# Attention scores on one core: output tiles of one head by four rows in place of two heads by eight

## The chip, the core and the metric

The kernel runs on one core of a Trainium2 chip. The core has a matrix engine (PE, TensorE), a vector engine (DVE, VectorE), a scalar engine (ACT, ScalarE), GpSimd (POOL), a queue engine that issues DMAs (SP, SyncE), and 16 DMA engines that move data between its on-chip memory and the chip's main memory. The metric is the device time of one execution in microseconds, lower is better. Before the change it is 205.95 us, the median of 3 runs (205.71 to 206.01).

## What is computed

For 8 batches and 8 heads, with 512 rows of 64 numbers each in q and k, all in float32, the kernel computes the scaled products of every row of q with every row of k:

```python
batch, heads, seq, dim = 8, 8, 512, 64
scale = 1.0 / np.sqrt(q.shape[-1])
return (np.einsum('bhqd,bhkd->bhqk', q, k) * scale).astype(np.float32)
```

The inputs are 16.8 MB together, the output is 67.1 MB.

## The kernel before

The work goes batch by batch. `load` (lines 53 to 58) brings k and q of one batch into two tiles of 1 MB: partition (g m) holds 16 consecutive rows (R = 16) of head g, and the same rows of head g + 4 (the index x is 0 or 1 for the two halves of the heads), so each partition receives two runs of 4 KB. Four batches (AHEAD = 4) are loaded ahead; the load of batch b + 4 is issued after the first pair of stores of batch b (line 131).

Then the data is cast to bf16 (line 87), on VectorE and ScalarE for the first batch and on GpSimd for all others. The cast puts the two heads of a pair side by side, so that one 128x128 transpose on PE (lines 95 and 103) turns both at once: afterwards partitions 0 to 63 hold the 64 numbers of head g and partitions 64 to 127 those of head g + 4. Eight transposes fill one PSUM tile, which VectorE copies into kT (line 97) and ScalarE into qT (line 105).

RO is the number of consecutive output rows that one partition of an output tile holds. All of these follow from it: HP = RO * 128 / 512, the number of heads that share the 128 partitions of an output tile; U = 128 / HP, the partitions per head; JJ = 16 / RO, how a query row is numbered inside qT; and IW = 8 / JJ, the rows i of qT that one copy fills. With RO = 8 they are HP = 2, U = 64, JJ = 2, IW = 4.

The matmuls (line 119) take a 64-row, U-column block of qT as weights and stream the 512 columns of kT. `tile_position` says which part of the 128x128 array is used: x chooses the upper or the lower 64 rows, h the columns. With U = 64 four matmuls cover the four quarters of the array. Two PSUM tiles of 128 x 2 x 512 are filled per step, one for each x; ScalarE evacuates and scales the first (line 71), VectorE the second (line 73). There are three such PSUM buffers, and two for the transposes.

Each pass over g0 (two heads for each x) fills two output tiles of 2 MB, one for each x, and then issues two stores (line 128) on SP's queue. There are six output buffers. A framework places the waits and orders the instructions of each engine from the data that they read and write; all DMAs stand on the one queue of SP in the order of the program.

Of the kernel before, what the change touches and what calls it, by code (L numbers as in the profile page):

```python
# [1 line left out]

# [5 lines left out]


@with_exitstack  # L10
def kernel(
    ctx: ExitStack,
    tc: tile.TileContext,
    q: bass.AP,
    k: bass.AP,
    out: bass.AP,
):

    nc = tc.nc
    B, H, S, D = q.shape
    scale = 1.0 / (D ** 0.5)
    P = 128
    G = H // 2
    M = P // G
    R = S // M
    RO = 8  # L30
    HP = RO * P // S
    U = P // HP
    JJ = R // RO

    f32 = mybir.dt.float32
    bf16 = mybir.dt.bfloat16

    q_r = q.rearrange("b (x g) (m j) d -> b (g m) x (j d)", x=2, j=R)
    k_r = k.rearrange("b (x g) (m j) d -> b (g m) x (j d)", x=2, j=R)
    out_r = out.rearrange("b (x n h) (u i) k -> b x n (h u) i k", x=2, h=HP, i=RO)  # L40

    consts = ctx.enter_context(tc.tile_pool(name="consts", bufs=1))
    raw_pool = ctx.enter_context(tc.tile_pool(name="raw", bufs=4))
    bf_pool = ctx.enter_context(tc.tile_pool(name="bf", bufs=2))
    t_pool = ctx.enter_context(tc.tile_pool(name="t", bufs=2))
    out_pool = ctx.enter_context(tc.tile_pool(name="out", bufs=6))
    tpsum_pool = ctx.enter_context(tc.tile_pool(name="tpsum", bufs=2, space=bass.MemoryType.PSUM))
    psum_pool = ctx.enter_context(tc.tile_pool(name="psum", bufs=3, space=bass.MemoryType.PSUM))

    AHEAD = 4  # L50
    raws = {}

    def load(b):
        kf = raw_pool.tile([P, 2, R * D], f32, name="kf")
        qf = raw_pool.tile([P, 2, R * D], f32, name="qf")
        nc.sync.dma_start(out=kf, in_=k_r[b])  # L56
        nc.sync.dma_start(out=qf, in_=q_r[b])
        raws[b] = (qf, kf)

    load(0)  # L60
    identity = consts.tile([P, P], dtype=bf16)
    make_identity(nc, identity)
    for b in range(1, AHEAD):
        load(b)

    n_evac = 0

    def evacuate(dst, src):
        nonlocal n_evac
        if n_evac % 2 == 0:  # L70
            nc.scalar.mul(out=dst, in_=src, mul=scale)  # L71
        else:
            nc.vector.tensor_scalar(out=dst, in0=src, scalar1=scale, scalar2=None,  # L73
                                    op0=mybir.AluOpType.mult)
        n_evac += 1

    for b in range(B):
        qf, kf = raws.pop(b)
        kb = bf_pool.tile([P, R, 2, D], bf16, name="kb")
        qb = bf_pool.tile([P, R, 2, D], bf16, name="qb")  # L80
        for slab, dst in ((kf, kb), (qf, qb)):
            for x in range(2):
                if b > 0:
                    copy = nc.gpsimd.tensor_copy
                else:
                    copy = (nc.vector.tensor_copy, nc.scalar.copy)[x]
                copy(out=dst[:, :, x, :], in_=slab[:, x].rearrange("p (j d) -> p j d", j=R))  # L87


        kT = t_pool.tile([P, P, R], bf16, name="kT")  # L90
        qT = t_pool.tile([P, RO, P, JJ], bf16, name="qT")
        for j0 in range(0, R, 8):
            tp = tpsum_pool.tile([P, 8, P], bf16, name="tp")
            for j in range(8):
                nc.tensor.transpose(out=tp[:, j, :], identity=identity,  # L95
                                    in_=kb[:, j0 + j].rearrange("p x d -> p (x d)"))
            nc.vector.tensor_copy(out=kT[:, :, j0:j0 + 8], in_=tp.rearrange("d j p -> d p j"))  # L97
        IW = 8 // JJ
        for i0 in range(0, RO, IW):
            tp = tpsum_pool.tile([P, IW, JJ, P], bf16, name="tp")  # L100
            for i in range(IW):
                for jj in range(JJ):
                    nc.tensor.transpose(out=tp[:, i, jj, :], identity=identity,  # L103
                                        in_=qb[:, RO * jj + i0 + i].rearrange("p x d -> p (x d)"))
            nc.scalar.copy(out=qT[:, i0:i0 + IW], in_=tp.rearrange("d i jj p -> d i p jj"))  # L105

        kTh = kT.rearrange("d (g m) j -> d g (m j)", g=G)
        qTh = qT.rearrange("d i (g m) jj -> d i g (m jj)", g=G)
        for g0 in range(0, G, 2):
            os = [out_pool.tile([P, 2 // HP, RO, S], f32, name="o") for _ in range(2)]  # L110
            for n in range(2 // HP):
                for i in range(0, RO, 2):
                    pss = [psum_pool.tile([P, 2, S], f32, name="ps") for _ in range(2)]
                    for w in range(2):
                        for h in range(HP):
                            g = g0 + n * HP + h
                            for x in range(2):
                                rows = slice(x * D, (x + 1) * D)
                                nc.tensor.matmul(out=pss[x][h * U:(h + 1) * U, w, :],  # L119
                                                 lhsT=qTh[rows, i + w, g, :],  # L120
                                                 rhs=kTh[rows, g, :],
                                                 start=True, stop=True,
                                                 tile_position=(x * D, h * U))
                    for x in range(2):
                        evacuate(os[x][:, n, i:i + 2, :], pss[x])
            for x in range(2):
                n0 = g0 // HP
                nc.sync.dma_start(  # L128
                    out=out_r[b, x, n0:n0 + 2 // HP].rearrange("n p i k -> p n (i k)"),
                    in_=os[x].rearrange("p n i k -> p n (i k)"))  # L130
            if g0 == 0 and b + AHEAD < B:
                load(b + AHEAD)


# [1 line left out]
_INS = ['q', 'k']  # L136
_OUTS = [((8, 8, 512, 512), 'float32')]


# [23 lines left out]
```

## Time and profile before

| what | value |
|---|---|
| median of 3 runs | 205.95 us |
| the profiled execution's own time | 205.95 us |
| its span | 204.0 us |
| instructions | 1911 |
| PE / VectorE / ScalarE / GpSimd busy | 63% / 46% / 41% / 14% of the span |
| DMA queue of SP | 8960 packets, 83.89 MB, 97.6% of 16 engines' span |
| a store of 2 MB, issue to landing | 24.8 us (32 of them) |
| a load of 1 MB, issue to landing | 17.2 us for k, 19.6 us for q (8 each) |

The page is taken from one execution. Its slices divide the span into 40 equal parts; a digit is the busy share in tenths. A group of instructions reads "line engine operation, out<-in, shapes, count | busy us, mean ns of one | idle time before them <- what ended it". A line of waits reads "engine, tile, line <- what it waited for: us in total, times, longest". The rows of a stretch give its start and end, its length, the busy us of PE, PE's weight loads, VectorE, ScalarE and GpSimd with their number of instructions, the granted clock of PE as a share of full speed, the mean busy share of the 16 DMA engines, and the rate at which they moved data. Busy shares are averages over stages; what a stage is worth is read from the wait that ends last in it.

### The profile page before, as it was taken

To read this page: it belongs to the slowest core of one execution; us is meant where nothing else is said; L and a number is where in the kernel's file an instruction comes from. 1 tells how busy PE (TensorE), PEld (TensorE's weight loads), DVE (VectorE), ACT (ScalarE), POOL (GpSimd) and SP (SyncE) were. 2 spreads that over 40 slices of the span, in tenths; PEclk is the share of its full clock that TensorE was granted. 3 is DMA by queue.
4 is the path that set the end of the run, shared out by engine and by line. 5 is a ranking of instruction groups with operands and counts; after the bars stand their busy time and mean duration, and the time that the engine had idled before them with its cause. 6 is when DMAs were issued, how large, how long until landed. Compare 5 with 4: busy or idle time off the path is not lost.

```text
span 204.0 us, 1911 instructions
## 1 busy us (share of the span) xinstructions
PE 128.7 (63%) x768; PEld 44.1 (22%) x768; DVE 94.4 (46%) x82; ACT 82.8 (41%) x83; POOL 29.0 (14%) x34
## 2 busy tenths in 40 slices
PE   0398877774969559696586955959787777600000
PEld 0353433260103411033110431103211111000000
DVE  0459895912639035490536705367628081800000
ACT  2477888263522625227252452527552525200000
POOL 1077530520006100070001600000000000000000
PEclk9999999666555855558555575555555555555555
DMA  5999999999999999999999999999999999999991
GB/s 204 419 409 411 439 427 404 441 434 424 437 400 432 440 421 419 434 429 427 440 407 414 438 427 437 427 421 437 424 430 437 426 434 424 430 437 427 434 408 61
DMA packets 8969, 84.01 MB, mean 412 GB/s; under 512 B 768, under 2 KB 768, under 8 KB 4864
## 3 DMA queue, kind: packets, MB, share of 16 engines
q1 hardware_dynamic: 8960, 83.89, 97.6%
q8 instruction: 6, 0.10, 0.2%
q14 instruction: 3, 0.02, 0.0%
HBM read 16.78 MB, written 67.11 MB: 411 GB/s over the span
## 4 chain that ended last, share of the span: by engine, by line
DMA 61%; DVE 14%; PE 6%; ACT 6%; issue 1%; SPq 0%; DVEq 0%
DMA out_dram<-o 57%; DVE o L73 11%; PE ps L119 4%; ACT o L71 4%; DMA qf<-in_q_dram 3%; DVE kT L97 3%; ACT qT L105 1%; PE tp L103 1%; PE tp L95 0%; DVE qb L87 0%; SPq L56 0%; SPq L128 0%; DVEq L73 0%
## 5 line engine op out<-in xcount | busy, mean ns | idle before, releaser
L119 PE MATMUL ps<-kT,qT 64*64 64x512 bf16 x512 | 103.1, 556 | 38.6 <-ACT o L71 24.9
L73 DVE TENSOR_SCALAR o<-ps 128x1024 f32<-128x1024 f32 x64 | 75.2, 1219 | 76.7 <-DMA out_dram<-o 56.8
L71 ACT ACTIVATE o<-ps 128x1024 f32<-128x1024 f32 x64 | 64.5, 1025 | 77.1 <-PE ps L119 65.7
L119 PEld LDWEIGHTS <-qT 64*64 64x64 bf16 x512 | 22.4, 124 | 111.5 <-issue 108.6
L87 POOL CAST kb<-kf 128x1024 bf16<-128x1024 f32 x14 | 14.2, 1040 | 80.9 <-DMA kf<-in_k_dram 80.3
L105 ACT COPY qT<-tp 128x1024 bf16<-128x1024 bf16 x16 | 16.1, 1015 | 12.6 <-PE tp L103 12.4
L97 DVE COPY kT<-tp 128x1024 bf16<-128x1024 bf16 x16 | 18.9, 1215 | 0.0
L95 PE MATMUL tp<-identity,kb 128*128 128x128 bf16 x128 | 12.4, 257 | 8.0 <-ACT kb L87 6.9
L103 PE MATMUL tp<-identity,qb 128*128 128x128 bf16 x128 | 14.9, 284 | 2.2 <-DVE kT L97 1.4
L87 POOL CAST qb<-qf 128x1024 bf16<-128x1024 f32 x14 | 14.2, 1040 | 6.4 <-DMA qf<-in_q_dram 6.4
L103 PEld LDWEIGHTS <-qb 128*128 128x128 bf16 x128 | 11.7, 130 | 9.6 <-issue 8.6
L95 PEld LDWEIGHTS <-kb 128*128 128x128 bf16 x128 | 10.4, 118 | 11.4 <-ACT kb L87 6.9
L87 DVE CAST kb<-kf 128x1024 bf16<-128x1024 f32 x1 | 0.7, 694 | 5.8 <-DMA kf<-in_k_dram 5.8
L87 ACT CAST kb<-kf 128x1024 bf16<-128x1024 f32 x1 | 1.0, 1044 | 3.8 <-DMA kf<-in_k_dram 3.8
L87 ACT CAST qb<-qf 128x1024 bf16<-128x1024 f32 x1 | 1.0, 1044 | 1.5 <-DMA qf<-in_q_dram 1.5
L87 ACT ACT_TABLE_LOAD x1 | 1.3, 1283 | 0.7 <-PEq L147 0.7
L87 DVE CAST qb<-qf 128x1024 bf16<-128x1024 f32 x1 | 0.7, 695 | 1.9 <-DMA qf<-in_q_dram 1.9
masks.py:199 POOL TENSOR_SCALAR_AFFINE_SELECT identity<-identity 128x128 bf16<-128x128 bf16 x1 | 0.3, 292 | 0.1
masks.py:197 POOL MEMSET identity<- 128x128 bf16 x1 | 0.2, 204 | 0.3 <-POOLq L147 0.3
L147 POOL MEMSET const-float32-0.0<- 128x1 f32 x1 | 0.1, 98 | 0.2 <-issue 0.2
L147 POOL MEMSET const-bfloat16-1.0<- 128x1 bf16 x1 | 0.1, 101 | 0.0
L147 POOL MEMSET const-uint8-127<- 128x1 uint8 x1 | 0.1, 101 | 0.0
(1 smaller groups left out, 0.1 us busy)
## 6 DMA issues: line engine op xcount, KB each, us to landing
out_dram<-o SPq DMA_DIRECT2D x32, 2048.0 KB, 24.8
kf<-in_k_dram SPq DMA_DIRECT2D x8, 1024.0 KB, 17.2
qf<-in_q_dram SPq DMA_DIRECT2D x8, 1024.0 KB, 19.6
```

The costliest lines, as they stand in the source:

```text
L71: nc.scalar.mul(out=dst, in_=src, mul=scale)
L73: nc.vector.tensor_scalar(out=dst, in0=src, scalar1=scale, scalar2=None, op0=mybir.AluOpType.mult)
L87: copy(out=dst[:, :, x, :], in_=slab[:, x].rearrange("p (j d) -> p j d", j=R))
L95: nc.tensor.transpose(out=tp[:, j, :], identity=identity, in_=kb[:, j0 + j].rearrange("p x d -> p (x d)"))
L97: nc.vector.tensor_copy(out=kT[:, :, j0:j0 + 8], in_=tp.rearrange("d j p -> d p j"))
L103: nc.tensor.transpose(out=tp[:, i, jj, :], identity=identity, in_=qb[:, RO * jj + i0 + i].rearrange("p x d -> p (x d)"))
L105: nc.scalar.copy(out=qT[:, i0:i0 + IW], in_=tp.rearrange("d i jj p -> d i p jj"))
L119: nc.tensor.matmul(out=pss[x][h * U:(h + 1) * U, w, :], lhsT=qTh[rows, i + w, g, :], rhs=kTh[rows, g, :], start=True, stop=True, tile_posi ...
L147: nc = _bacc.Bacc("TRN2", target_bir_lowering=False, num_devices=1)
```

## The change

One constant is changed:

```diff
-    RO = 8
+    RO = 4
```

All else follows from it. HP becomes 1, U 128, JJ 4 and IW 2. An output tile is 128 x 2 x 4 x 512 in place of 128 x 1 x 8 x 512: the same 2 MB, but the two heads of a pass stand one behind the other in each partition, four rows (8 KB) of each, where before each half of the partitions held eight rows (16 KB) of one head. A store therefore writes 256 runs of 8 KB in place of 128 runs of 16 KB. The loop over n now runs twice and the loop over i over 0 and 2 in place of 0, 2, 4 and 6, so the number of steps (four in a pass) and of evacuations stays. The weights of a matmul are 64 rows by 128 columns in place of 64 by 64, so a step has four matmuls in place of eight, each on one half of the array. In qT the index jj has 4 values in place of 2, and one copy fills 2 values of i in place of 4; the number and size of the copies stay.

## The prediction

> **What bounds the kernel now.** I read the page's 40 slices first, then the DMA packets and queue, then the chain, and last the waits, to see who is early and who is late.
>
> ```profile
> DMA  5999999999999999999999999999999999999991
> GB/s 204 419 409 411 439 427 404 441 434 424 437 400 432 440 421 419 434 429 427 440 407 414 438 427 437 427 421 437 424 430 437 426 434 424 430 437 427 434 408 61
> DMA packets 8969, 84.01 MB, mean 412 GB/s; under 512 B 768, under 2 KB 768, under 8 KB 4864
> q1 hardware_dynamic: 8960, 83.89, 97.6%
> ```
>
> The DMA row is full from the second slice to the last but one: the 16 DMA engines are never out of work. The queue's 8960 packets take 97.6% of 16 engines' span. They divide into 768 tiny ones (16 completion marks for each of 48 transfers), 4096 under 8 KB (the loads: 16 x 128 partitions x 2 runs of 4 KB) and the rest, 4096 store runs of 16 KB.
>
> ```profile
> DMA out_dram<-o 57%; DVE o L73 11%; PE ps L119 4%; ACT o L71 4%; DMA qf<-in_q_dram 3%; DVE kT L97 3%; ACT qT L105 1%; PE tp L103 1%; PE tp L95 0%; DVE qb L87 0%; SPq L56 0%; SPq L128 0%; DVEq L73 0%
> L119 PE MATMUL ps<-kT,qT 64*64 64x512 bf16 x512 | 103.1, 556 | 38.6 <-ACT o L71 24.9
> L73 DVE TENSOR_SCALAR o<-ps 128x1024 f32<-128x1024 f32 x64 | 75.2, 1219 | 76.7 <-DMA out_dram<-o 56.8
> POOL kb L87 <- DMA kf<-in_k_dram: 80.3, 6, 20.0
> DVE o L73 <- DMA out_dram<-o: 56.8, 11, 8.7
> ```
>
> The chain (first line) is mostly stores, and the waits (last two) say the same from the other side: VectorE stands 56.8 us because the output buffers are still being stored, and GpSimd 80.3 us because loads queue behind stores. The 14% of evacuation in the chain is no compute bound: it is the refill after a buffer comes free, with other stores still in flight above it. So what counts is how long the 16 engines need for their packets, and the moments at the two ends when they have none. The third view is the busy time in chosen stretches:
>
> ```profile
> core 0: us, PE busy (x) PEld busy (x) DVE busy (x) ACT busy (x) POOL busy (x), PEclk, DMA share, GB/s
> 4.00:22.00 18.00, 12.62 (x128) 7.68 (x128) 12.14 (x12) 11.23 (x12) 8.80 (x9) 1.00 1.03 413
> 120.00:190.00 70.00, 42.97 (x196) 9.85 (x195) 30.53 (x26) 25.67 (x26) 0.00 (x0) 0.52 1.01 430
> 197.00:200.00 3.00, 0.00 (x0) 0.00 (x0) 0.00 (x0) 0.00 (x0) 0.00 (x0) 0.50 0.66 284
> 200.00:204.00 4.00, 0.00 (x0) 0.00 (x0) 0.00 (x0) 0.00 (x0) 0.00 (x0) 0.50 0.10 41
> ```
>
> The first stretch holds loads alone (4 KB packets), the second stores alone (16 KB). Both are gapless (a share over 1 is packets that overlap a little), yet 413 GB/s against 430: **the size of a packet has a price here.** The last two rows show that the engines don't end together: from 197 us the share falls, and some engines go on for 4 us more. By the landings of the last store the 16 engines finish 4.4 us apart, and the latest one sets the end.
>
> **The change, part by part.**
>
> *Store runs.* With RO = 4 a partition of an output tile holds two runs of 4 rows (8 KB), one for each of two heads, in place of one run of 16 KB. Still 32 stores of 2 MB, but 8192 packets for 4096. Per engine: 256 packets of 16 KB become 512 of 8 KB, 256 more. What does one more packet cost? In the trace's packet records the median 16 KB store takes 611 ns and the median 4 KB load 159 ns. If a packet is a fixed part a plus bytes at one rate, 4 x 159 - 611 = 25 = 3a, so a = 8.3 ns and 8 KB take (611 + 8.3) / 2 = 310 ns. The rates agree: 4096 x 16 / 413 = 158.7 and 16384 x 16 / 430 = 609.6 give a = 8.4. There is a third witness: of the eight 8 KB packets in the trace (instruction fetches, another queue) the shortest take 309 ns. So 256 x 8.3 ns = **+2.1 us**. No cover hides it, because the DMA engines are what everything waits for. Bounds, as no row shows an 8 KB store: below, the fixed part may belong to loads only, 0 us. Above, the means (163.9 and 612.9 ns) give a = (4 x 163.9 - 612.9) / 3 = 14.2 ns, +3.6 us; the far end is the median of the eight fetches, 352 ns: 256 x (2 x 352 - 611) = +24 us, but those ran between others' packets. I take 2.1, as two rates and the 309 ns agree on it.
>
> [...]
>
> *Latest engine.* One engine's store packets take some 15 ns more than 611 while the compute engines run, about 3.3 us by the end, and instruction fetches delay single engines by 0.3 to 1 us each; thus the 4.4 us. The matmul line falls from 512 matmuls and 512 weight loads to 256 of each, so the program from 1911 to about 1400 instructions. If what slows that engine goes with the instruction count, it loses 27% of 3.3 = 0.9 us; but the next latest engine ends only 0.8 us sooner, so the gain ends there unless it loses a fetch too. Bounds 0 and -1.2; I take **-0.3**, nearer to nothing, as no row shows what slows it.
>
> *Matmuls.* Per pair of evacuations 8 matmuls on quarters of the array become 4 on halves. Before, four start within 10 ns of each other, and the next four 427 ns later at the low clock. Eight take 0.63 us in one place and 1.08 in another:
>
> ```profile
> 17.18 0.63 PE L119 MATMUL ps<-kT,qT 64*64 64x512 bf16 x8 [0.37 <-ACT o L71]
> 18.89 0.84 SPq L128 DMA_DIRECT2D out_dram<-o  x2
> 145.62 1.08 PE ps L119 x8
> ```
>
> Two halves side by side stream as many columns, so the same 1.1 us. No row shows halves. Bound above: nothing overlaps, 4 x 0.43 + 4 x 0.13 of weight load + 0.2 = 2.4 us. A batch is 8 such groups and 32 transposes (16 take 2.10 us in the timeline): 8 x 2.4 + 4.2 = 23.4 us. Its DMA takes 8.39 MB at 430 and 2.10 MB at 413 GB/s: 19.5 + 5.1 = 24.6 us. Even so it is hidden in steady state. At the start, the first two stores are issued at 18.89 us, while 8.39 MB of loads at 413 GB/s last from 2.3 to 22.6: 3.7 us of cover, against 4 x (2.4 - 1.1) = 5.2 in that worst case, so at most 1.5 us lost. By likely overlap: 0. The other way, a faster start gains nothing: the engines are still loading.
>
> *Copies and evacuations.* qT is written in groups of 4 rather than 2, kT as before; 64 + 64 evacuations of 128x1024 stay. ACT's 1.015 us copy may move by some tenths; 16 of them lie in 77 us of idle ScalarE. The built order puts the second batch's first kT and qT copies behind the first four evacuations, which brings the first store forward by about one 1.2 us copy; the loads in flight cover that. Cost 0.
>
> *SyncE.* A store carries 256 runs, as a load does (median issue 0.49 us for a store's 0.34): 32 x 0.15 us on a queue that mostly waits. Issue blocks sooner if the queue counts packets, but then work is queued by definition. Cost 0.
>
> Sum, against the profiled execution's own 205.95 us (span 204.0, which is also the median of the three runs): 205.95 + 2.1 - 0.3 = **207.8 us**.
>
> **Rivals.**
>
> *The halves cost nothing (not slower).* An engine streams 8 KB in 305.5 ns, the fixed part being a cost of reads. For it: only reads show small packets. Against it: then the bytes alone would go at 16384 / 611 = 26.8 bytes a ns in stores and at 4096 / (159 - a) in loads, two rates where the 309 ns packet fits one. Then 205.95 with 0 to -1.2: 204.8 to 206.0. It decides if the median store packet is 306.9 ns or less: 512 x (306.9 - 305.5) = 0.7 us, less the 0.3 of the engine term.
>
> *Stores to two heads at once are slower in memory.* Consecutive runs of one partition now lie 1 MB apart, not in one 16 KB row. For it: mixed stretches have packets of 164 to 172 ns. Against it: a load's two runs lie 512 KB apart and it holds 413 GB/s, and neighbouring partitions still lie side by side. From a = 14 ns up: 209.6, up to 229.8 with 352 ns a packet. [...]
>
> *The change does not do what it says*: runs are cut to 4 KB, as in loads. Then 768 more packets an engine x 8.3 = 6.4 us: 212.3. The built program names 128x2x2048 elements per store, which speaks against it.
>
> *Matmul halves that do not overlap*: +1.5 us at the start at worst, 209.3 with the packets.
>
> **How the numbers follow.** Forecast case (a from 5 to 14 ns, engine term 0 to -1.2), 206.0 to 209.6: 0.74. Costless halves: 0.12. Slower memory: 0.09; runs cut: 0.02; serial halves: 0.03, most of it inside the forecast's span. The range 206.0 to 209.7 keeps the forecast, the serial halves and a part of the costless case's top. This kernel's measurement can tell about 0.2% (0.4 us) from no change. Faster: half of the costless case, 0.06. Same: the other half and the bottom of the forecast (small a, large engine term), 0.10. Slower: 0.84.
>
> **What would show it.** Right: 8192 store packets, median 309 to 311 ns; stores alone at 423 to 424 GB/s (8192 x 16 / 310); the DMA row still full; VectorE still waiting for out_dram; matmul groups of four in 0.6 and 1.1 us. Wrong: 430 GB/s in the store stretch (costless), below 415 (memory), a slice under 9 near 20 to 30 us (start starved), or landings of the last store more than 6 us or less than 2 us apart, which would mis-size the engine term.

## The result and the profile after

The change made the kernel slower: 208.12 us, the median of four runs (207.73 to 208.35), against 205.96 us before (205.71 to 206.01). The ratio is 1.0105, 95% interval 1.0087 to 1.0124. The profiled execution took 208.35 us with a span of 206.4 us; instructions fell from 1911 to 1399.

First the page of the kernel after: the DMA row and the rate in 40 slices, packets, SP's queue, the chain by line and the two largest groups.

```profile
DMA  5999999999999999999999999999999999999991
GB/s 207 420 410 409 429 427 403 425 430 430 429 400 402 429 429 415 417 422 427 422 421 388 424 427 427 430 429 425 430 425 424 425 429 425 427 425 424 424 398 62
DMA packets 13063, 83.98 MB, mean 407 GB/s; under 512 B 768, under 2 KB 768, under 8 KB 4864
q1 hardware_dynamic: 13056, 83.89, 97.7%
...
DMA out_dram<-o 52%; PE ps L119 11%; DVE o L73 9%; DMA qf<-in_q_dram 3%; PE tp L103 3%; PE tp L95 3%; DVE kT L97 2%; ACT o L71 1%; ACT qT L105 1%; DVE qb L87 0%; SPq L56 0%; DVEq L73 0%
L119 PE MATMUL ps<-kT,qT 64*128 64x512 bf16 x256 | 103.1, 601 | 33.9 <-ACT o L71 20.7
L73 DVE TENSOR_SCALAR o<-ps 128x1024 f32<-128x1024 f32 x64 | 75.7, 1221 | 77.6 <-DMA out_dram<-o 58.1
```

The DMA engines are again busy from the second slice to the last but one, 4096 store packets more go through them (13056 for 8960), and VectorE still waits for stores (58.1 us for 56.8). But the rate has dips that the even part of the change does not explain: slices 7, 12, 13 and 22, at 403, 400, 402 and 388 GB/s, where loads and stores meet. Before, only slices 7 and 12 were as low (404 and 400). Next come chosen stretches of the kernel after: loads alone, stores alone and the end (start and end, length, busy us of PE, PE's weight loads, VectorE, ScalarE and GpSimd, PE's clock, DMA share, GB/s):

```profile
core 0: us, PE busy (x) PEld busy (x) DVE busy (x) ACT busy (x) POOL busy (x), PEclk, DMA share, GB/s
4.00:22.00 18.00, 13.45 (x71) 6.10 (x72) 9.88 (x10) 9.48 (x10) 8.83 (x9) 1.00 1.03 413
120.00:190.00 70.00, 42.04 (x116) 7.94 (x113) 30.38 (x26) 26.11 (x27) 0.00 (x0) 0.52 1.01 427
200.00:203.00 3.00, 0.00 (x0) 0.00 (x0) 0.00 (x0) 0.00 (x0) 0.00 (x0) 0.50 0.48 202
203.00:206.40 3.40, 0.00 (x0) 0.00 (x0) 0.00 (x0) 0.00 (x0) 0.00 (x0) 0.50 0.09 39
```

Loads alone go as before (413). Stores alone go at 427, where my 310 ns a packet would give 423. The last landings of the 16 engines lie 4.4 us apart, for 4.5 before.

Landings tell the pace better than durations do: each of the 16 engines marks the end of its part of a transfer (768 marks for 48 transfers in both traces), and I take the earliest of the 16 marks. In a stretch of stores alone it comes every 4.862 us for 2 MB in 16 KB packets and every 4.900 in 8 KB packets; the first loads, of 1 MB each, land every 2.560 us in both kernels. So 8 packets more in a store cost 38 ns, **4.7 ns each, not 8.3**, and all 256 cost 1.2 us. The other 1.2 us of the profiled execution's 2.4 were not in my sum. The experiments look for them.

### The profile page after: what moved, and what is told of

Its sections match the earlier page's. It is cut to its first block, busy times and chain, and to the rows that moved or that the text cites. A ratio compares the mean times of both kernels' runs of the same rounds, so it can differ in the third digit from the quotient of the medians.

```text
span 206.4 us, 1399 instructions
## 1 busy us (share of the span) xinstructions
PE 134.1 (65%) x512; PEld 42.0 (20%) x512; DVE 95.0 (46%) x82; ACT 83.1 (40%) x83; POOL 29.1 (14%) x34
## 3 DMA queue, kind: packets, MB, share of 16 engines
q1 hardware_dynamic: 13056, 83.89, 97.7%
## 4 chain that ended last, share of the span: by engine, by line
DMA 56%; PE 16%; DVE 12%; ACT 3%; issue 0%; SPq 0%; DVEq 0%
DMA out_dram<-o 52%; PE ps L119 11%; DVE o L73 9%; DMA qf<-in_q_dram 3%; PE tp L103 3%; PE tp L95 3%; DVE kT L97 2%; ACT o L71 1%; ACT qT L105 1%; DVE qb L87 0%; SPq L56 0%; DVEq L73 0%
## 5 line engine op out<-in xcount | busy, mean ns | idle before, releaser
L119 PE MATMUL ps<-kT,qT 64*128 64x512 bf16 x256 | 103.1, 601 | 33.9 <-ACT o L71 20.7
L73 DVE TENSOR_SCALAR o<-ps 128x1024 f32<-128x1024 f32 x64 | 75.7, 1221 | 77.6 <-DMA out_dram<-o 58.1
L119 PEld LDWEIGHTS <-qT 64*128 64x128 bf16 x256 | 15.9, 106 | 107.5 <-issue 103.5
L95 PE MATMUL tp<-identity,kb 128*128 128x128 bf16 x128 | 16.4, 304 | 8.7 <-ACT kb L87 6.9
L103 PE MATMUL tp<-identity,qb 128*128 128x128 bf16 x128 | 17.0, 307 | 2.8 <-DVE kT L97 1.4
L95 PEld LDWEIGHTS <-kb 128*128 128x128 bf16 x128 | 13.3, 142 | 15.2 <-issue 8.1
L103 PEld LDWEIGHTS <-qb 128*128 128x128 bf16 x128 | 13.1, 139 | 13.8 <-issue 10.7
```

Of the source, the lines that this page charges most:

```text
L95: nc.tensor.transpose(out=tp[:, j, :], identity=identity, in_=kb[:, j0 + j].rearrange("p x d -> p (x d)"))
L119: nc.tensor.matmul(out=pss[x][h * U:(h + 1) * U, w, :], lhsT=qTh[rows, i + w, g, :], rhs=kTh[rows, g, :], start=True, stop=True, tile_posi ...
```

## The experiments

Both kernels write the same 2 MB block with each store; what differs is which partition writes which piece of it, and in what lengths. Below, "places" means this: before, neighbouring partitions write 16 KB apart; after, they write 8 KB apart, and the two pieces of one partition lie 1 MB apart.

The theory at this point: a fixed cost for each packet, all of it on the path that sets the end. The rivals: (A) the new places in memory are slow, as I thought by the jump of 1 MB between the two heads of a partition; (B) the matrix engine, with 128-column weights, is slower.

### Packets alone, 8 KB and 4 KB

The kernel before keeps its rows and places, but the output tile gets 128 bytes of unused space between pieces of C rows, so a store's packets are cut there.

```diff
-os = [out_pool.tile([P, 2 // HP, RO, S], f32, name="o") for _ in range(2)]
+C = 4   # 2 in the second kernel
+os = [out_pool.tile([P, RO // C, C * S + 32], f32, name="o") for _ in range(2)]
...
-out=out_r[b, x, n0:n0 + 2 // HP].rearrange("n p i k -> p n (i k)"),
-in_=os[x].rearrange("p n i k -> p n (i k)"))
+out=out_r[b, x, n0].rearrange("p (c i) k -> p c (i k)", i=C),
+in_=os[x][:, :, :C * S])
```

> The kernel before (RO = 8, four quarters, one head after the other in memory), with 128 bytes of unused space between the two 8 KB halves of a partition's output row, so that a store is cut into 8 KB packets that lie side by side in memory. Theory (a fixed cost per packet, 7 to 8.3 ns, and every packet on the path that sets the end): 4096 more packets, 256 an engine, 1.8 to 2.1 us, so 207.8 to 208.1 us, median store packet 309 ns. Rival A (runs of one partition 1 MB apart are slow): nothing of that is here, so 206.0. Rival B (128-column weights, the matrix engine slower): nothing of that is here, so 206.0.

> The same with the partition's 16 KB cut into four runs of 4 KB. Theory: 768 more packets an engine than before, each 7 to 8.3 ns: +5.4 to +6.4 us, so 211.4 to 212.3 us, median store packet 157 to 159 ns, and the cost grows in proportion to the packets. If the cost were of the second run alone, or of the gap in the partition, it would be near 208.

With 8 KB packets (13056 on SP's queue for 8960): 206.48 us, ratio 1.0023 (1.0014 to 1.0033), so +0.5 us. With 4 KB (21248): 209.15 us, ratio 1.0148 (1.0134 to 1.0162), +3.2 us. The packet's median duration is the expected 309 and 159 ns in both, yet the time is a quarter and a half of what those durations said. The landings of the earliest engine come every 4.900 and 4.975 us: 38 ns for 8 more packets, 113 ns for 24, again 4.7 ns. In the profiled executions the mean of the last landings moved by 1.0 us from before to 8 KB; the latest engine, which sets the end, moved by only 0.5. **Number and size of packets explain some 0.5 of the change's 2.2 us in the time, and about 1 us of a typical engine's path.** The first theory falls as the whole cause.

### The matrix engine: quarters again

The kernel after, each matmul cut into two of 64 columns:

```diff
-for h in range(HP):
-    g = g0 + n * HP + h
+for h in range(2):
+    g = g0 + n
...
-nc.tensor.matmul(out=pss[x][h * U:(h + 1) * U, w, :],
-                 lhsT=qTh[rows, i + w, g, :],
+nc.tensor.matmul(out=pss[x][h * D:(h + 1) * D, w, :],
+                 lhsT=qTh[rows, i + w, g, h * D:(h + 1) * D],
...
-                 tile_position=(x * D, h * U))
+                 tile_position=(x * D, h * D))
```

> The kernel after, with each matmul cut into two with 64-column weights, so that four quarters of the array work at once as before, and the instruction count is again that of before (1911). Stores are as after: 8 KB runs. Theory: 208.1 us as after, within 0.3 us, though the first store is issued near 19 us in place of 20.4. Rival B (the slower matrix engine is what costs): 206.0 to 206.5.

207.87 us, ratio 1.0091 (1.0077 to 1.0105): the cost stays with the quarters back. Rival B falls. One part of the expectation failed: the first store was issued at 20.7 us, not near 19, so that delay does not come from the halves.

### The jump of 1 MB

The kernel after, with each store issued as two of 1 MB, one head each:

```diff
-nc.sync.dma_start(
-    out=out_r[b, x, n0:n0 + 2 // HP].rearrange("n p i k -> p n (i k)"),
-    in_=os[x].rearrange("p n i k -> p n (i k)"))
+for n in range(2):
+    nc.sync.dma_start(
+        out=out_r[b, x, n0 + n].rearrange("p i k -> p (i k)"),
+        in_=os[x][:, n].rearrange("p i k -> p (i k)"))
```

> The kernel after with each store issued as two of 1 MB, one head each: still 8192 packets of 8 KB, but each transfer writes one block of 1 MB without a gap, and no packet is followed by one 1 MB away within a transfer. Theory: 208.1 us, plus 32 more completion marks an engine at 9 ns, 0.3 us: 208.1 to 208.5. Rival A (the jump of 1 MB costs): 206.0 to 206.5.

207.84 us, ratio 1.0095 (1.0075 to 1.0115). The jump inside a transfer is not what costs. So it is neither the packets alone, nor the matmuls, nor the jump. What else differs between the padded kernel and these three is the rest of the places, neighbouring partitions 8 KB apart in place of 16, the order of the work, and the padded kernel's gap of 128 bytes on the chip.

### More instructions

The engine term of the prediction, weighed in the kernel before by issuing every matmul twice (`for h in [0, 1, 0, 1]`); the second overwrites the first with the same numbers.

> The kernel before with every matmul and its weight load issued twice (the second overwrites the first with the same numbers): 512 more matmuls and 512 more weight loads, the stores unchanged at 16 KB. It weighs the engine term of the prediction: if the latest of the 16 engines is late in proportion to the instructions (3.3 us for 1911), 1024 more make it 1.8 us later, and the time 206.3 to 207.8. If it is not, and the matrix engine has the slack that I reckoned, 205.9 to 206.2.

208.28 us, ratio 1.0119 (1.0098 to 1.0140). More instructions do cost, more than I reckoned, but mostly not by the engine term: the median engine lands the loads of the fifth batch 1.3 us later (39.5 us for 38.2), following a slice at 345 GB/s, and only 1.0 us is added by the latest engine's distance from the mean at the end. A term of that kind is there all the same: from the last loads to the end the latest engine's distance from the median grows by 2.3 us here, by 0.3 in the kernel before. Still, the 0.9 us that I hoped to gain from fewer instructions isn't confirmed, and the slack of the start is smaller than I reckoned.

### The DMAs alone

Four kernels issue the loads and stores in the order of the program, without any compute; the stores write a constant tile, and wait for nothing that is computed. (The lines of casts, transposes, matmuls and evacuations, all taken out, are not shown.)

```diff
+o = out_pool.tile([P, 2 // HP, RO, S], f32, name="o")
+nc.vector.memset(o, 0.0)
 for b in range(B):
     for g0 in range(0, G, 2):
         for x in range(2):
             n0 = g0 // HP
             nc.sync.dma_start(
                 out=out_r[b, x, n0:n0 + 2 // HP].rearrange("n p i k -> p n (i k)"),
-                in_=os[x].rearrange("p n i k -> p n (i k)"))
+                in_=o.rearrange("p n i k -> p n (i k)"))
         if g0 == 0 and b + AHEAD < B:
             load(b + AHEAD)
```

The four differ in RO (8, 4 or 16) and in the padding; with RO = 16 a store is 4 MB. A fifth, last, has RO = 4 and stores of one head, as in the split above.

> The DMAs alone: the loads and stores of the kernel before in their order (16 KB runs), with no casts, transposes, matmuls or evacuations; the stores write a constant tile, so the scores are not computed. It gives the floor. From the landings of one engine in the kernel before (2.49 us a load, 4.86 us a store): 16 x 2.49 + 32 x 4.86 = 195.4 us, and with 2.1 us ahead of the first data and some 2 us of launch and end, 199 to 202 us. How far it lies below 206.0 is what the compute engines' activity adds.

> The DMAs alone with 8 KB packets, the two of a partition side by side in memory (as in the padded kernel); no scores are computed. Revised theory (4.7 ns for one more packet, by the landings of one engine: 4.862 us a store of 16 KB runs, 4.900 of 8 KB, 4.975 of 4 KB): 1.2 us more than with 16 KB runs. First theory (8.3 ns): 2.1 us more.

> The DMAs alone in the places of the kernel after: 8 KB packets, two heads in a partition, neighbouring partitions 8 KB apart; no scores are computed. If the places in memory cost something (rival A in a weaker form), this is 0.5 to 1.2 us slower than the padded form; if what is left of the change's cost comes from the compute engines' order, the two are the same within 0.3 us.

> The DMAs alone with 32 KB runs and 16 stores of 4 MB; no scores are computed. Revised theory: 128 packets an engine fewer at 4.7 ns and 16 completion marks fewer, 0.6 to 0.7 us less than with 16 KB runs. Then the slower time of the full kernel with 32 KB runs is one of supply at its start, not of its packets.

> The DMAs alone in the places of the kernel after, but each store issued as two of 1 MB, one head each, so that no 8 KB packet is followed by one 1 MB away in its transfer and neighbouring partitions still lie 8 KB apart; no scores are computed. It splits the cost of the places. If the jump of 1 MB costs: as the padded form, 203.5 us, or 0.2 more for the added completion marks. If it is that the 16 engines write 64 KB apart (8 partitions x 8 KB) in place of 128 KB: 205 to 206, as the form with two heads.

| stores (no compute) | median us | range | ratio to the whole kernel before |
|---|---|---|---|
| 16 KB runs, places of before | 203.92 | 202.62 to 204.27 | 0.9889 (0.9869 to 0.9910) |
| 8 KB, padded, places of before | 203.45 | 203.16 to 203.74 | 0.9873 (0.9860 to 0.9887) |
| 8 KB, places of after | 206.02 | 204.76 to 206.71 | 0.9992 (0.9975 to 1.0008) |
| 8 KB, places of after, 1 MB stores | 206.65 | 204.95 to 207.25 | 1.0015 (0.9994 to 1.0037) |
| 32 KB runs | 201.98 | 201.67 to 202.46 | 0.9804 (0.9790 to 0.9819) |

With no compute at all, and the same number of packets of the same size, **the places of after cost 2.6 us more than the padded form** (206.02 - 203.45, where I had expected 0.5 to 1.2), and removing the jump removes nothing (206.65). One thing besides the places differs, the gap of 128 bytes on the chip. If that gap helped by itself, the first row, which has no gap, gives a lower bound: 206.02 - 203.92 = 2.1 us, of which the packets take 1.2 by landings (4.900 us a store in both forms, for 4.862), so the places cost 0.9 or more.

The packets by themselves do not show in the time between the first two rows, where I had expected 1.2 or 2.1 us; they do show in the median engine's way from the first landing to the last, 193.6 against 194.7 us. Two more expectations missed: the first row lies above the 199 to 202 us that I had reckoned, and 32 KB runs gain 1.9 us on it in place of 0.6 to 0.7 (0.4 between the two traced executions).

Where the places cost is seen in three stretches, one with loads among the stores, one of stores alone, and one near the end (columns: start and end, length, VectorE, GpSimd, PE's clock, DMA share, GB/s). First the padded form:

```profile
107.00:117.00 10.00, 0.00 (x0) 0.00 (x0) 1.00 1.02 426
130.00:165.00 35.00, 0.00 (x0) 0.00 (x0) 1.00 1.01 428
184.00:194.00 10.00, 0.00 (x0) 0.00 (x0) 1.00 1.02 430
```

Then the places of after:

```profile
107.00:117.00 10.00, 0.00 (x0) 0.00 (x0) 1.00 1.02 413
130.00:165.00 35.00, 0.00 (x0) 0.00 (x0) 1.00 1.01 428
184.00:194.00 10.00, 0.00 (x0) 0.00 (x0) 1.00 1.01 423
```

And two whole kernels (columns as in the first fence of stretches), the padded one with 8 KB packets and then the kernel after:

```profile
107.00:117.00 10.00, 8.00 (x42) 2.45 (x40) 6.97 (x6) 2.36 (x3) 3.55 (x4) 0.50 1.03 420
130.00:165.00 35.00, 27.20 (x128) 6.78 (x128) 16.80 (x16) 16.92 (x17) 0.00 (x0) 0.50 1.01 426
184.00:194.00 10.00, 0.00 (x0) 0.00 (x0) 0.00 (x0) 0.00 (x0) 0.00 (x0) 0.50 1.01 428
```

```profile
107.00:117.00 10.00, 7.19 (x17) 1.08 (x16) 5.85 (x6) 3.28 (x4) 2.03 (x2) 0.50 1.01 403
130.00:165.00 35.00, 27.00 (x75) 5.32 (x74) 18.00 (x16) 16.92 (x18) 0.00 (x0) 0.50 1.01 427
184.00:194.00 10.00, 0.00 (x0) 0.00 (x0) 0.00 (x0) 0.00 (x0) 0.00 (x0) 0.50 1.02 426
```

In the middle, stores alone go equally fast in all four (428, 428, 426 and 427 GB/s), so a steady stretch shows nothing of this cost. It is lost where loads pass between stores (426 to 413 GB/s without compute, 420 to 403 in the whole kernels). In the packet records a load packet takes 159 ns as a rule; of the 1536 of the last three batches, those over 200 ns are none in the padded form and 42 in the places of after, the longest 945 ns. In the whole kernels they are 17 before, 14 in the padded kernel and 68 after. The last five or six stores are slower as well, 4.98 us each for 4.90 (in the kernel after the last four, 4.98 to 5.03), and only in the places of after. How far the latest engine lands behind the median one shows who pays (us, in the DMAs alone, when the last load of these batches has landed, and at the end):

| | batch 3 | batch 4 | batch 5 | batch 6 | batch 7 | end |
|---|---|---|---|---|---|---|
| 16 KB, places of before | 0.4 | 0.5 | 0.4 | 0.5 | 0.8 | 0.9 |
| 8 KB, padded | 0.3 | 0.4 | 0.3 | 0.3 | 0.3 | 0.4 |
| 8 KB, places of after | 0.5 | 0.4 | 0.9 | 2.2 | 3.4 | 3.1 |

With the places of after, the latest engine falls back at the loads of batches 5, 6 and 7, by 0.4 to 1.3 us each time, and has not caught up at the end. A rate that is a mean over 16 engines hides this; the end of the kernel is the latest engine's: in both kernels the span ends 0.83 us after its last mark. The table shows the direction better than the size: each row is one traced execution, the last row the slowest of its twelve (206.71 us), the other two the fastest of theirs (202.62 and 203.16).

In the whole kernels the latest engine lies far behind in any case, 3.5 us at the end before, 3.2 in the padded kernel and 4.1 after. From the padded kernel to the kernel after, the median engine ends 0.9 us later and the latest 1.9, so there the cost falls on both.

### Longer runs

RO = 16: four heads by 16 rows in a tile, 32 KB runs, 4 MB stores, three output buffers, one x after the other with 32-column weights. The second kernel stores the first batch's tiles in halves.

```diff
-RO = 8
+RO = 16
...
+for x in range(2):
+    o = out_pool.tile([P, RO, S], f32, name="o")
+    for i in range(0, RO, 2):
+        ps = psum_pool.tile([P, 2, S], f32, name="ps")
...
+        evacuate(o[:, i:i + 2, :], ps)
+        c = 8 if b == 0 else 16     # 16 throughout in the first kernel
+        if (i + 2) % c == 0:
+            nc.sync.dma_start(
+                out=out_r[b, x, 0][:, i + 2 - c:i + 2].rearrange("p i k -> p (i k)"),
+                in_=o[:, i + 2 - c:i + 2].rearrange("p i k -> p (i k)"))
```

> RO = 16: four heads by 16 rows in an output tile, runs of 32 KB, stores of 4 MB, 32-column weights, one half of the heads (x) after the other, three output buffers of 4 MB. Theory: 128 fewer packets an engine than before, 0.9 to 1.1 us less, so 204.9 to 205.1 us if the engines stay supplied; the risk is the start, where the first 4 MB tile needs about 8.5 us of matmuls and would be issued near 22 us, as the loads run out (about 22.6 us): up to 1 us of idle engines. Rival A and rival B: 206.0 or slower, as neither has a gain here.

> The kernel with 32 KB runs, but the first batch's tiles are stored in two halves (16 KB runs) as soon as each half is evacuated, so that the first store is issued near 18 us in place of 22. If only the start held back the 32 KB runs: 207.9 less the 1.3 to 1.5 us that their packets lost at 31 to 39 us, so 206.0 to 206.6, and at best 204.5 to 205.5 with the gain that the DMAs alone show (1.8 us). If it stays at 207.9, the half-used matrix engine supplies the stores too late in later batches too.

207.93 us, ratio 1.0096 (1.0080 to 1.0111), and 206.99 us, ratio 1.0048 (1.0035 to 1.0061). The DMAs alone with 32 KB runs took 201.98, so there is room for a gain, but neither kernel reaches it, and both missed what I expected (204.9 to 205.1, and 206.0 to 206.6). In the first of the two the engines run short soon after the first store; these are its stretches in the columns of the whole kernels:

```profile
28.00:32.00 4.00, 3.37 (x30) 1.46 (x27) 2.77 (x3) 2.63 (x4) 0.50 (x1) 1.00 1.10 393
32.00:36.00 4.00, 3.53 (x36) 1.71 (x39) 2.68 (x3) 1.45 (x2) 1.52 (x2) 1.00 0.67 264
```

The share falls to 0.67 while PE is busy 3.53 of 4 us. Storing halves at the start brings back 0.9 us, and the median engine then ends where it does in the kernel before (199.66 us for 199.69). What is left is the latest engine, 4.3 us behind the median for 3.5 before and 0.9 in the DMAs alone with 32 KB runs; no run shows why. Neither is faster than the kernel before.

## Why the prediction was right, and where it was not

The time was forecast at 207.8 and came out at 208.1; the direction was right, and so was what bounds the kernel. That the sum came so near was luck: two errors nearly cancel, the packets too dear and the places at nothing.

1. *What bounds the kernel.* Right. DMA packets set the end in both kernels, and with all compute gone the time falls by only 2 us (203.92).
2. *Store runs, +2.1 us.* This term was mis-sized: "a = 8.3 ns" is 4.7 ns, so 1.2 us on an engine's path, and in the time of the padded kernel 0.5. I took the durations of packets as if one began where the last ended. They overlap: store packets of 16, 8 and 4 KB are recorded with 611, 309 and 159 ns, but the landings leave 607.8, 306.3 and 155.5 for each, some 3 ns less, and 4 x 159 - 611 counts that overlap three times. The DMA share of 1.03 in the stretch of loads and 1.01 in that of stores said so on my own fence. The check by rates agreed for another reason. It set loads against stores, and a load packet is dearer than a store packet of the same 4 KB: the first loads land every 2.560 us, which is 160.0 ns for each of an engine's 16 packets, against 155.5. My lower bound, "the fixed part may belong to loads only", allowed for a part of this. So the 8.3 by durations and the 8.4 by rates were no witnesses for each other. The forecast's range began at 5 ns a packet, which no row of before shows; the landings of three sizes gave 4.7, 1.2 us in the sum in place of 2.1. What in the engine takes the 4.7 ns, no run shows.
3. *The rival on places in memory* had 0.09 and was named for the wrong reason. Its evidence against, "neighbouring partitions still lie side by side", is the very thing that changed: they lie 8 KB apart in place of 16. Its price, 209.6 and more, was for a cost in every packet; the cost is at the loads and at the end. It is 2.6 us without compute, and up to 1.6 in the whole kernels (208.12 - 206.48), where the order of the work differs too. So a step that I gave little chance makes up as much as three quarters of what was measured.
4. *Latest engine, -0.3 us.* Not seen: the last landings lie 4.5 us apart before and 4.4 after. The reading behind it, 15 ns more for each store packet of one engine, does not show in the landings of the kernel before either. From 116 to 154 us, with stores alone, the earliest and the latest stay 3.6 us apart. The distance grows in steps: 1.2, 0.9 and 0.8 us at loads that land at 25, 65 and 115 us, and 0.6 us at 164.
5. *Matmuls, 0.* Right in the time. Groups of four halves take as long as eight quarters at a granted clock of 0.50, 1.07 us here for 1.08 before:

```profile
147.93 1.07 PE ps L119 x4
```

But two halves start every 0.40 us from 12 to 35 us, where before two or four quarters started every 0.215 us between 17 and 35 us (medians). The granted clock was 1.00 up to 35 us in both and does not tell them apart. The first store was issued at 20.43 us in place of 18.89; the loads in flight until 23 us covered that.

6. *Copies, evacuations, SyncE, 0.* Nothing contradicts it, but the expectation that the first store would come forward by a copy of 1.2 us was wrong.

What stays open: why places 8 KB apart are slow where loads and stores meet and at the end, and whether the distance that matters is that of partitions or of the engines' larger blocks; no run changed one without the other, and none shows which partitions an engine serves (the 64 KB in one expectation is an assumption). Nor is it settled why the DMAs alone take no more time with 8 KB than with 16 KB runs, when the median engine needs 1.1 us more; the latest engine was closer to the others in the run with 8 KB, and the trace with 16 KB is of the fastest execution of six (202.62 us, the others 203.76 to 204.27). The padded form's gap of 128 bytes on the chip was not tried by itself, so the share of the places lies between the bound of 0.9 us and the 2.6 that the padded form gives.

## What to carry to other kernels

Where DMA is the bound, take the pace from landings or from a long stretch of one kind, not from packet durations (here 607.8 ns for a 16 KB store packet by landings, 611 by duration), and compare stores with stores and not with loads. Ask of a new layout three things apart: how many packets, how long each run, and how far apart the places are that are written at the same time. Test the last with the DMAs alone and a padded twin that has the same packets in the old places: five small kernels told here what the whole kernel could not. Here the time was that of the latest of the 16 engines, 3.5 us behind the median one before and 4.1 after, so look at each load among stores, not only at the steady rate.

## What the hardware showed that I had not expected

- One store packet more costs 4.7 ns at 4, 8 and 16 KB alike, by landings (4.975, 4.900 and 4.862 us for 2 MB), and 4 MB of 32 KB runs take 9.671 us, which fits to 0.02 us (in the DMAs alone 434 GB/s from 130 to 165 us).
- A load packet of 4 KB takes 160.0 ns of an engine's pace when loads go alone, a store packet of 4 KB 155.5.
- The same 8 KB packets in other places (and without the gap on the chip) cost 2.6 us of 204, seen where loads pass and in the last five or six stores; the steady stretch is the same to 1 GB/s (428 and 428 without compute, 426 and 427 in the whole kernels).
- The DMAs alone need 203.9 of the 206.0 us of the whole kernel; all casts, transposes, matmuls and evacuations add 1%.
